# Block sums of the two right-hand operands made and split early, kept in DRAM, and loaded by GpSimd's queue

## The chip, the cores and the metric

The kernel runs on one core of one Trainium2 chip. The metric is the device time of one execution in microseconds (us). TensorE (PE) does the matmuls, and its weight loads are listed apart as PEld; VectorE is DVE, ScalarE is ACT, GpSimd is POOL, and SyncE (SP) does little but issue DMAs. DMAs issued from SP go to a hardware queue, those issued from GpSimd to a software queue; GpSimd also computes.

## The reference, cut to what matters

One layer of a hybrid block on 1024 tokens of 1024 channels, all in float32:

```python
h = rms_norm(x, norm_g)
z = h @ w_in                       # 1024 x 9216: q, k, v, gate of retention; q, k, v, gate of
                                   # differential attention; two merge gates mg_r, mg_d
o_r = rms_norm(retention(q_r, k_r, v_r), ret_norm_g) * silu(gate_r)      # chunks of 128
o_d = rms_norm(diff_attention(qd, kd, v_d), sub_norm_g) * silu(gate_d)   # causal, ALiBi
m = sigmoid(mg_r) * (o_r @ ret_w_o) + sigmoid(mg_d) * (o_d @ diff_w_o)
out = x + m @ w_out
```

## The kernel before, in words

**Split operands.** A float32 matrix is used in matmuls as two parts in the type float32r, a high part (an ACT copy) and a low part (a DVE subtraction of the high part from the original). `split` and `cut` make them; each takes one ACT and one DVE instruction for 128 x 512 numbers. A product is the sum of three passes, high x high, high x low and low x high, so one `product` of 128 x 512 results over 512 rows is 4 x 3 = 12 matmuls.

**The order of stages.** The normalised input, transposed, stays in SBUF as `hT`, four tiles `hq[kh, f]` (kh: which half of the 1024 channels, f: which half of the tokens), each of 128 partitions x 4 row blocks x 2 parts x 512 tokens (16 KB per partition). Then come the projections `rqk0`, `rv0`, `rqk1`, `rv1` of the retention (two groups of four heads, eight token tiles each), with the retention's own small matmuls put between them by hand (`after` gives an item a tick and a weight, `among` lays it between the parts of a projection). After these come the eight heads of the attention in the same manner, with the projections of the gates begun beside them (`first_duo`). Then follow three groups of large products: the gate projections of `h` (16 pairs), the two branch projections `y` (`ret_w_o`, then `diff_w_o`), and the output projection `out` with `w_out`.

**The large products** save matmuls by a scheme with sums of blocks. The right-hand operand R is seen as 2 x 2 blocks r11, r12, r21, r22, and these are used instead of them:

```python
t1 = r11 + r12;  t3 = r12 + r22;  t2 = r22 + t1;  t4 = t2 + r21
```

Each of these is a split tile of the size of an `hq`. Seven products are made for each pair of output strips: two "firsts" (with r11 and r21) and five "rests" (with t2, t3, t1, then t4 and r22). For the gates R is `hT`; for `y0` and `y1` it is the gated branch output `og`, read from DRAM; for `out` it is `w_out`. A dictionary `RB` holds the tiles in use, and `HOME` gives each a fixed place: r11, t3, r21, r22 lie where the four `hq` were, and t1, t2, t4 in a pool `act2`, which is opened when the attention's pools are closed. So there is one place for each name, and a new tile waits until the old one has been read for the last time.

`late_r(name, src)` makes the t tiles from DRAM through staging tiles, or, with no `src` (the gates), from the two parts of the `hq` in place. `early_r` loads and splits r11 and r21. `firsts` and `rests` run the products; `Pair.prep` loads a pair's left operand (two raw tiles of the tag `wraw`, three buffers), makes four sums of its blocks on DVE and splits them. For a strip of `y`, `done_y` loads the gate `s` (and, in the last pair of the second branch, the running sum `m`), both through two buffers of the tag `ld`, multiplies, and either stores to `md` from SP or accumulates into `md` by a DMA from GpSimd's queue. The firsts of `out` read `md` back (`rf_out`).

**The order on each engine** is set by a planner that simulates the program before it is built: it fills each engine's and each queue's list in the order in which instructions become ready in its simulation, earlier program lines first. Each engine and each queue then takes its list strictly in order. So instructions of `out` stand among those of `y1`, where their inputs allow it.

In the retention `r_qkT`, `r_kv`, `r_state`, `r_score`, `r_o` and `r_out` handle one tile of 128 tokens of four heads; the values `v` of a tile have eight buffers, the squares `sq` two.

Of the kernel before, what the change touches and what calls it, by code (L numbers as in the profile page):

```python
# [9 lines left out]
F32 = mybir.dt.float32  # L10
F32R = mybir.dt.float32r
AF = mybir.ActivationFunctionType
ALU = mybir.AluOpType
AX = mybir.AxisListType

P = 128
# [46 lines left out]
def tile_hybrid_block(ctx, tc, x, norm_g, w_in, ret_norm_g, ret_w_o, dq_g, dk_g,  # L63
                      lq1, lk1, lq2, lk2, sub_g, diff_w_o, w_out, consts, out):
    nc = tc.nc
    x, w_in, out = x[0], w_in[0], out[0]
    ret_w_o, diff_w_o, w_out = ret_w_o[0], diff_w_o[0], w_out[0]
# [4 lines left out]
    dram = ctx.enter_context(tc.tile_pool(name="dram", bufs=1, space=bass.MemoryType.DRAM))  # L72
    wpool = ctx.enter_context(tc.tile_pool(name="wpool", bufs=NWS))
    gp = ctx.enter_context(tc.tile_pool(name="gp", bufs=3))
# [6 lines left out]
    def split(t, src):  # L81

        n = src.shape[-1]
        nc.scalar.activation(t[:, 0, :n], src, AF.Copy)
        nc.vector.tensor_tensor(t[:, 1, :n], src, t[:, 0, :n].bitcast(F32), ALU.subtract)
# [94 lines left out]
    md = [dram.tile([P, 4, S], F32, name=f"md{kh}") for kh in range(2)]  # L180
    first = [dram.tile([P, 2, 512], F32, name=f"first{q}") for q in range(16)]


    def cols(c, n):
        return w_in[:, c:c + n]
# [35 lines left out]
    def first_duo(q, following):  # L221

        banks = [pst("pj", f"fb{q + i}") for i in range(2)]
        for kh in range(2):
# [13 lines left out]
    hq = {(q, f): act.tile([P, 4, 2, 512], F32R, tag=f"r{q}{f}", name=f"hT{q}{f}")  # L238
          for f in range(2) for q in range(2)}
    hT = {(k, f): hq[k // 4, f][:, k % 4] for f in range(2) for k in range(NK)}  # L240

    def proj(chunk, t, n=512):
        if t == 3:
            wnext(chunk)
        z = pst("pj", f"z_{chunk}_{t}")
        step(z[:, :n], [hT[k, t // 4] for k in range(NK)], slice((t % 4) * P, (t % 4 + 1) * P),
             W[chunk], slice(0, n))
        return z

    with tc.tile_pool(name="rq", bufs=8) as rq, ExitStack() as early:  # L250
# [34 lines left out]
        R = {}  # L285

        def qk_unit(g, t):
            z = proj(f"rqk{g}", t)
            qk = rq.tile([P, 512], F32, tag="qk", name=f"qk{g}{t}")
            nc.vector.tensor_tensor(  # L290
                qk.rearrange("p (a b) -> p a b", b=64), z.rearrange("p (a b) -> p a b", b=64),
                qkdec[:, g, :].unsqueeze(2).broadcast_to([P, 8, 64]), ALU.mult)
            R[g, t] = dict(qk=qk)
            tick()
# [10 lines left out]
        rp = early.enter_context(tc.tile_pool(name="rp", bufs=2))  # L305
# [30 lines left out]
        nc.vector.tensor_tensor(nlam, ls[:, 3:4], ls[:, 2:3], ALU.subtract)  # L336
        nc.vector.tensor_scalar(nlam, nlam, -LAM_INIT, None, ALU.add)

        def r_qkT(g, t):
            c = R[g, t]  # L340
            tp = pst("tr", f"qkTp{g}{t}", NTR)
            for j in range(4):
                nc.tensor.transpose(tp[:, j * P:(j + 1) * P], c["qk"][:, j * P:(j + 1) * P], ident)

            qz = c["qz"] = qzs[t % 3]
            for e in range(2):
                b = slice(64 * e, 64 * e + 64)
                nc.scalar.activation(qz[b, e::2, :], tp[b, :256].rearrange("p (a b) -> p a b", b=P),
                                     AF.Copy)
            kT = c["kT"] = rp.tile([P, 2, 256], F32R, tag="kT", name=f"kT{g}{t}")  # L350
            split(kT, tp[:, 256:])
            qs = c["qs"] = rp.tile([P, 2, 512], F32R, tag="qs", name=f"qs{g}{t}", bufs=QSB)
            qf = qz.rearrange("p a b -> p (a b)")
            nc.scalar.activation(qs[:, 0, :], qf, AF.Copy)
            nc.gpsimd.tensor_tensor(qs[:, 1, :], qf, qs[:, 0, :].bitcast(F32), ALU.subtract)
# [41 lines left out]
        def r_o(g, t):  # L397
            c = R[g, t]
            o = pst("s", f"ro{g}{t}")
            for h in range(4):  # L400
                hsl = slice(h * P, (h + 1) * P)
                nc.tensor.matmul(o[:, hsl], c["sT"][:, h, :], c["v"][:, hsl],
                                 start=True, stop=(t == 0))
                if t > 0:
                    nc.tensor.matmul(o[:, hsl], c["qz"][:, h, :],
                                     R[g, t - 1]["state"][:, h // 2, :], start=False, stop=True)
            sq = rp.tile([P, 4, P], F32, tag="sq", name=f"rsq{g}{t}")
            nc.scalar.activation(sq.rearrange("p a b -> p (a b)"), o, AF.Square)
            ss = rp.tile([P, 8], F32, tag="ss", name=f"rss{g}{t}")
            nc.vector.tensor_reduce(ss[:, :4], sq, AX.X, ALU.add)  # L410
            rstd(ss[:, 4:], ss[:, :4], rp, f"r{g}{t}", 4, 1.0 / P)
            o1 = c["o"] = rp.tile([P, 4, P], F32, tag="o1", name=f"ro1{g}{t}")
            nc.vector.tensor_tensor(o1, o.rearrange("p (a b) -> p a b", b=P),
                                    ss[:, 4:].unsqueeze(2).broadcast_to([P, 4, P]), ALU.mult)
# [12 lines left out]
        for g in range(2):  # L427
            if g > 0:
                for t in range(NT):
                    qk_unit(g, t)  # L430
            for t in range(NT):
                z = proj(f"rv{g}", t)
                if t == 0:
                    group_consts(g)
                v = R[g, t]["v"] = rp.tile([P, 512], F32, tag="v", name=f"v{g}{t}", bufs=8)
                nc.scalar.activation(v, z, AF.Copy)
                after(1, .46, lambda a=(g, t): r_qkT(*a))
                if t < NT - 1:
                    after(1, .01, lambda a=(g, t): r_kv(*a))
                    after(2, .64, lambda a=(g, t): r_state(*a))  # L440
                after(2, .64, lambda a=(g, t): r_score(*a))
                after(3, 1.72, lambda a=(g, t): r_o(*a))
                after(5, .46, lambda a=(g, t): r_out(*a))
                tick()
# [14 lines left out]
    with tc.tile_pool(name="dp", bufs=2) as dp:  # L459
# [175 lines left out]
        for q in range(4, 12, 2):  # L635
# [14 lines left out]
                t1=(act2, "t1"), t2=(act2, "t2"), t4=(act2, "t4"))  # L650

    def new_r(which, name):
        pool, tag = HOME[which]
        RB[which] = pool.tile([P, 4, 2, 512], F32R, tag=tag, name=f"{which}_{name}")
        return RB[which]
# [5 lines left out]
    def cut_r(which, j, src):  # L661
        t = RB[which]
        cut(t[:, j, 0, :], t[:, j, 1, :], src)

    def add(dst, a, b, op=ALU.add):
        nc.vector.tensor_tensor(dst, a, b, op)  # L666

    def stage(name):
        return lpool.tile([P, 512], F32, tag="rs", name=name, bufs=7)

    def whole(which, j):

        return RB[which][:, j, 0, :].bitcast(F32), RB[which][:, j, 1, :].bitcast(F32)

    def early_r(name, src):

        for which, kh in (("r11", 0), ("r21", 1)):
            new_r(which, name)
            for j in range(4):
                r = stage(f"{which}_{name}{j}")  # L680
                nc.sync.dma_start(r, src(kh, j, 0))
                cut_r(which, j, r)

    def late_r(name, src):

        for n in ("t2", "t1", "t4"):
            new_r(n, name)
        if src:
            new_r("t3", name)
        for j in range(4):  # L690
            r11, r12, r22 = (stage(f"{n}_{name}{j}") for n in ("r11s", "r12s", "r22s"))
            for r, kh, f, which in ((r11, 0, 0, "r11"), (r12, 0, 1, "t3"), (r22, 1, 1, "r22")):
                if src:
                    nc.sync.dma_start(r, src(kh, j, f))
                else:
                    add(r, *whole(which, j))
            add(r11, r11, r12)
            add(r12, r12, r22)
            add(r22, r22, r11)
            cut_r("t2", j, r22)  # L700
            cut_r("t3", j, r12)
            cut_r("t1", j, r11)
        if src:
            new_r("r22", name)
        for j in range(4):
            t = stage(f"t4_{name}{j}")
            if src:
                r22 = stage(f"r22t_{name}{j}")
                nc.sync.dma_start(t, src(1, j, 0))
                nc.sync.dma_start(r22, src(1, j, 1))  # L710
                h, l = whole("t2", j)
                add(t, t, h)
                add(t, t, l)
            else:
                add(t, *whole("t2", j))
                for half in whole("r21", j):
                    add(t, t, half)
            cut_r("t4", j, t)
            if src:
                cut_r("r22", j, r22)  # L720

    def run(parts):
        for part in parts:
# [167 lines left out]
    def o_src(br):  # L891
        return lambda kh, j, f: og[br][kh][:, j, f * 512:(f + 1) * 512]

    late_r("h", None)
    first_duo(12, lambda: more(14, 15))
    pairs = [gate_pair(q) for q in range(16)]
    first_duo(14, pairs[0].prep)
# [29 lines left out]
        rests([Pair(f"y{br}{p}", srcs[p], lambda t=p1[p]: t, done_y(p)) for p in range(4)])  # L927


    def w_src(kh, j, f):  # L930
        return w_out[(4 * kh + j) * P:(4 * kh + j + 1) * P, f * 512:(f + 1) * 512]

    def m_src(i):
        def src(kh, s0, n):
            return md[kh].rearrange("p j (s i n) -> p j s i n", s=2, i=4)[:, :, s0:s0 + n, i, :]
# [11 lines left out]
    def first_out(i, b):  # L947
        done_out(i)(0, 0, temp("c", f"c11_out{i}"), b)

    early_r("w", w_src)  # L950
    p1 = firsts("out", [m_src(i) for i in range(4)], first_out)
    late_r("w", w_src)
    rests([Pair(f"out{i}", m_src(i), lambda t=p1[i]: t, done_out(i)) for i in range(4)])


# [24 lines left out]
```

## Time and profile before

| what | value |
|---|---|
| median of 3 runs (lowest, highest) | 1325.26 us (1324.67, 1328.49) |
| the profiled execution | 1325.96 us, of which its span is 1324.2 us |
| mean granted clock of TensorE over the span | 0.985 of full |
| PE busy / DVE busy / ACT busy / POOL busy | 1260.6 / 954.6 / 647.4 / 265.3 us |
| moved by DMA | 171.01 MB, mean 129 GB/s |
| of that on SP's queue / on GpSimd's queue | 165.78 MB / 3.95 MB |

Busy time is the time in which an engine executes; matmuls overlap their neighbours, so a busy PE is not a PE at its peak. The stages on the span's clock, about: norm and `rqk0` to 72 us, the retention to 290, the attention to 794, the gates from there, `y0` and `y1` until 1240, `out` to the end. "DMA share" is the mean busy share of the core's 16 DMA engines in a stretch.

### The profile page before, as it was taken

To read this page: it belongs to the slowest core of one execution; us is meant where nothing else is said; L and a number is where in the kernel's file an instruction comes from. 1 tells how busy PE (TensorE), PEld (TensorE's weight loads), DVE (VectorE), ACT (ScalarE), POOL (GpSimd) and SP (SyncE) were. 2 spreads that over 40 slices of the span, in tenths; PEclk is the share of its full clock that TensorE was granted. 3 is DMA by queue.
4 is the path that set the end of the run, shared out by engine and by line. 5 is a ranking of instruction groups with operands and counts; after the bars stand their busy time and mean duration, and the time that the engine had idled before them with its cause. 6 is when DMAs were issued, how large, how long until landed. Compare 5 with 4: busy or idle time off the path is not lost. (4 is left out here: it accounts for less than half of the span.)

```text
span 1324.2 us, 19831 instructions
## 1 busy us (share of the span) xinstructions
PE 1260.6 (95%) x6836; PEld 1112.0 (84%) x6836; DVE 954.6 (72%) x2020; ACT 647.4 (49%) x1448; POOL 265.3 (20%) x367
## 2 busy tenths in 40 slices
PE   7999999999999999999999995999989999999598
PEld 5888888889999999999999884787767777778487
DVE  7436435736786878778686849987665799998884
ACT  6235123527575766757576633433433554333430
POOL 3134113323342524334242100000000000011000
PEclk9999999999999999999999998999999999999799
DMA  7212120331020201202020544687655768979864
GB/s 258 59 37 72 57 72 8 116 115 49 1 65 9 56 15 51 64 1 65 9 72 9 169 158 159 219 279 242 208 189 170 248 213 265 324 208 256 255 199 144
DMA packets 158262, 171.01 MB, mean 129 GB/s; under 512 B 9920, under 2 KB 108368, under 8 KB 158160
## 3 DMA queue, kind: packets, MB, share of 16 engines
q1 hardware_dynamic: 155904, 165.78, 39.1%
q0 software_dynamic: 2256, 3.95, 2.0%
q8 instruction: 54, 0.88, 0.3%
q14 instruction: 48, 0.39, 0.1%
HBM read 123.55 MB, written 46.14 MB: 128 GB/s over the span
## 5 line engine op out<-in xcount | busy, mean ns | idle before, releaser
L121 PE MATMUL z_d<-w_d,hT 128*128 128x384 f32 x1536 | 300.7, 340 | 0.7 <-DVE nsq L486 0.7
L121 PEld LDWEIGHTS z_d<-w_d,hT 128*128 128x128 f32 x1536 | 264.2, 188 | 2.8 <-DVE nsq L486 1.0
L537 ACT ACTIVATE S<-S,ast 128x256 f32<-128x256 f32 (+7 forms) x128 | 98.7, 772 | 29.2 <-DVE ast L533 27.6
L531 PE MATMUL sps<-K,Q 128*128 128x512 f32 (+5 forms) x384 | 107.9, 364 | 0.3 <-ACT Q L512 0.3
L121 PE MATMUL z_rv<-w_rv,hT 128*128 128x512 f32 x384 | 98.8, 398 | 0.0
L918 POOL DMA_DIRECT2D md<-c_y x12 | 10.5, 872 | 433.4 <-DVE c_y L909 422.3
L121 PE MATMUL z_rqk<-w_rqk,hT 128*128 128x512 f32 x384 | 95.0, 401 | 1.4 <-ACT hT L281 1.4
L130 PE MATMUL fb<-hT,fw 128*128 128x512 f32 x384 | 94.3, 396 | 0.9 <-ACT ft L229 0.9
L121 PEld LDWEIGHTS z_rqk<-w_rqk,hT 128*128 128x128 f32 x384 | 71.6, 192 | 16.3 <-ACT hT L281 2.0
L130 PEld LDWEIGHTS fb<-hT,fw 128*128 128x128 f32 x384 | 70.3, 188 | 14.9 <-ACT ft L229 1.1
L571 PE MATMUL dops<-V,aTs 128*128 128x128 f32 x576 | 81.8, 276 | 0.0
L571 PEld LDWEIGHTS dops<-V,aTs 128*128 128x128 f32 x576 | 78.5, 191 | 2.6
L121 PEld LDWEIGHTS z_rv<-w_rv,hT 128*128 128x128 f32 x384 | 68.7, 188 | 11.7
L533 DVE CUSTOM_DVE_ANT_0 S<-sps,ndist 128x512 f32<-128x512 f32 (+5 forms) x128 | 67.5, 534 | 5.1 <-PE sps L531 4.7
L91 POOL TENSOR_TENSOR nss<-ms_n,mh 128x4 f32<-128x4 f32 x64 | 65.9, 1029 | 4.1
L531 PEld LDWEIGHTS sps<-K,Q 128*128 128x128 f32 x384 | 63.3, 190 | 2.2 <-ACT Q L512 0.9
L488 POOL TENSOR_TENSOR nsq<-nsq,gh 128x256 f32<-128x256 f32 x64 | 50.2, 788 | 73.4 <-DVE nsq L486 62.0
L130 PE MATMUL y_h<-t_h,ls_h 128*128 128x512 f32 x192 | 48.6, 401 | 15.1 <-ACT ls_h L658 15.1
L130 PE MATMUL w_h<-t_h,l_h 128*128 128x512 f32 x192 | 48.6, 404 | 10.0 <-DVE u_h L823 9.1
L548 DVE SCALAR_TENSOR_TENSOR S<-S,ast,S 128x128 f32<-128x128 f32 (+3 forms) x64 | 56.6, 884 | 1.3
L130 PEld LDWEIGHTS y_h<-t_h,ls_h 128*128 128x128 f32 x192 | 37.1, 194 | 23.9 <-ACT ls_h L658 15.5
L130 PEld LDWEIGHTS w_h<-t_h,l_h 128*128 128x128 f32 x192 | 36.3, 192 | 20.8 <-DVE u_h L823 12.1
(246 smaller groups left out, 2721.5 us busy)
## 6 DMA issues: line engine op xcount, KB each, us to landing
wr_d<-in_w_in_dram SPq DMA_DIRECT2D x96, 128.0 KB, 2.7
fr<-in_w_in_dram SPq DMA_DIRECT2D x16, 512.0 KB, 4.4
first<-ft SPq DMA_DIRECT2D x32, 256.0 KB, 2.2
ra_h<-in_w_in_dram SPq DMA_DIRECT2D x16, 512.0 KB, 3.6
rb_h<-in_w_in_dram SPq DMA_DIRECT2D x16, 512.0 KB, 5.1
s<-sg SPq DMA_DIRECT2D x32, 256.0 KB, 4.4
og<-c_h SPq DMA_DIRECT2D x24, 256.0 KB, 3.3
sg<-c_h SPq DMA_DIRECT2D x24, 256.0 KB, 3.2
```

The source lines that it names most:

```text
L91: nc.gpsimd.tensor_tensor(out_t, ms, mh[:, :n], ALU.pow)
L121: nc.tensor.matmul(o, a[k][:, i0, asl], b[k][:, i1, bsl], start=(k == 0 and j == 0), stop=(k == NK - 1 and j == 2))
L130: nc.tensor.matmul(bank, L[:, i0, j * P:(j + 1) * P], R[:, j, i1, :], start=(start and j == 0 and i == 0), stop=(j == 3 and i == 2), skip_ ...
L488: nc.gpsimd.tensor_tensor(sq, sq, hd["g"], ALU.mult)
L531: nc.tensor.matmul(sp[:, :m], hd["Q"][t][:, j, e, :], hd["K"][:, j, c], start=(e == 0), stop=(e == 1))
L533: nc.vector.tensor_tensor_reduce(sb[:, c], sp[:, :m], ndist[:, S - n + m * f:S - n + m * f + m], -slope, FMAX if f == 0 else st[:, j:j + 1 ...
L537: nc.scalar.activation(sb[:, :n], sb[:, :n], AF.Exp, bias=st[:, j:j + 1], scale=-1.0, accum_out=st[:, 2 + j:3 + j])
L548: nc.vector.scalar_tensor_tensor(S0[:, :n], S1[:, :n], st[:, 6:7], S0[:, :n], ALU.mult, ALU.add)
L571: nc.tensor.matmul(o[:, :P], aT[:, b, :], hd["V"][f][:, b, :], start=(kb == 0), stop=(kb == t))
L918: nc.gpsimd.dma_start(m, t, accum_op=ALU.add)
```

## The change

The sums t1 to t4 of `hT`, and all seven right-hand tiles of `w_out`, are made during the retention by a new function `r_ahead`. For each row block `j` it makes the sums on DVE in float32, splits each (ACT and DVE) into one of three buffers of the tag `oq`, and stores the 512 KB from GpSimd's queue into a DRAM tile `ahead`. `hT` is handled beside `rv0` (after the token tiles 1, 3, 5 and 7), `w_out` beside `rqk1`; the raw blocks of `w_out` are loaded by SP. Where the tiles are used, `load_r` loads them from DRAM by GpSimd's queue, two DMAs of 1 MB for a tile. `late_r` is now for `og` alone and `early_r` for `og` alone; the `hT` sum t3 gets a tile of its own at its home and is no longer written over `hq[0, 1]`. To make room, `v` has five buffers and `sq` one. The diff, with lines left out that only follow from this:

```diff
+    ahead = {(n, w): dram.tile([P, 4, 2, 512], F32R, name=f"{w}_{n}")
+             for w, ns in (("h", ("t1", "t2", "t3", "t4")),
+                           ("w", ("r11", "r21", "r22", "t1", "t2", "t3", "t4"))) for n in ns}
...
+        op = early.enter_context(tc.tile_pool(name="op", bufs=2))
+
+        def put(n, w, j, src):
+            o = op.tile([P, 2, 512], F32R, tag="oq", name=f"oq_{w}{n}{j}", bufs=3)
+            split(o, src)
+            nc.gpsimd.dma_start(ahead[n, w][:, j], o)
+
+        def r_ahead(w, j):
+            def tt(o, a, b):
+                nc.vector.tensor_tensor(o, a, b, ALU.add)
+            def raw(n, j):
+                if n == "r21":
+                    return op.tile([P, 512], F32, tag="or", name=f"or_{n}{j}", bufs=1)
+                return gp.tile([P, 512], F32, tag="gt", name=f"or_{w}{n}{j}", bufs=3)
+            q = {}
+            for n, (kh, f) in dict(r11=(0, 0), r12=(0, 1), r22=(1, 1), r21=(1, 0)).items():
+                if w == "w":
+                    q[n] = raw(n, j)
+                    nc.sync.dma_start(q[n], w_out[(4 * kh + j) * P:(4 * kh + j + 1) * P,
+                                                  f * 512:(f + 1) * 512])
+                    if n != "r12":
+                        put(n, w, j, q[n])
+                elif n != "r21":
+                    q[n] = raw(n, j)
+                    tt(q[n], *(hq[kh, f][:, j, i, :].bitcast(F32) for i in range(2)))
+            tt(q["r11"], q["r11"], q["r12"])
+            put("t1", w, j, q["r11"])
+            tt(q["r12"], q["r12"], q["r22"])
+            put("t3", w, j, q["r12"])
+            tt(q["r22"], q["r22"], q["r11"])
+            put("t2", w, j, q["r22"])
+            for r in ([q["r21"]] if w == "w" else [hq[1, 0][:, j, i, :].bitcast(F32) for i in range(2)]):
+                tt(q["r22"], q["r22"], r)
+            put("t4", w, j, q["r22"])
...
-            sq = rp.tile([P, 4, P], F32, tag="sq", name=f"rsq{g}{t}")
+            sq = rp.tile([P, 4, P], F32, tag="sq", name=f"rsq{g}{t}", bufs=1)
...
                     qk_unit(g, t)
+                    if t % 2 == 1:
+                        r_ahead("w", t // 2)
             for t in range(NT):
                 z = proj(f"rv{g}", t)
+                if g == 0 and t % 2 == 1:
+                    r_ahead("h", t // 2)
...
-                v = R[g, t]["v"] = rp.tile([P, 512], F32, tag="v", name=f"v{g}{t}", bufs=8)
+                v = R[g, t]["v"] = rp.tile([P, 512], F32, tag="v", name=f"v{g}{t}", bufs=5)
...
+    def load_r(name, which, queue):
+        for n in which:
+            t = new_r(n, name)
+            for j in range(0, 4, 2):
+                queue.dma_start(t[:, j:j + 2], ahead[n, name][:, j:j + 2])
...
-    late_r("h", None)
+    load_r("h", ("t3", "t2", "t1", "t4"), nc.gpsimd)
...
-    early_r("w", w_src)
+    load_r("w", ("r11", "r21", "t2", "t3", "t1", "t4", "r22"), nc.gpsimd)
     p1 = firsts("out", [m_src(i) for i in range(4)], first_out)
-    late_r("w", w_src)
     rests([Pair(f"out{i}", m_src(i), lambda t=p1[i]: t, done_out(i)) for i in range(4)])
```

More of the change, by code (lines that the diff above doesn't have):

```diff
@@ L684, in late_r @@
     def late_r(name, src):
-        for n in ("t2", "t1", "t4"):
+        for n in ("t2", "t3", "t1", "t4"):
             new_r(n, name)
-        if src:
-            new_r("t3", name)
         for j in range(4):
             r11, r12, r22 = (stage(f"{n}_{name}{j}") for n in ("r11s", "r12s", "r22s"))
[L692 to L696, printed above, removed]
+            for r, kh, f in ((r11, 0, 0), (r12, 0, 1), (r22, 1, 1)):
+                nc.sync.dma_start(r, src(kh, j, f))
             add(r11, r11, r12)
@@ L702, in late_r @@
             cut_r("t1", j, r11)
-        if src:
-            new_r("r22", name)
+        new_r("r22", name)
         for j in range(4):
[L706 to L717, printed above, removed]
-            cut_r("t4", j, t)
-            if src:
-                cut_r("r22", j, r22)
+            t, r22 = stage(f"t4_{name}{j}"), stage(f"r22t_{name}{j}")
+            nc.sync.dma_start(t, src(1, j, 0))
+            nc.sync.dma_start(r22, src(1, j, 1))
+            for half in whole("t2", j):
+                add(t, t, half)
+            cut_r("t4", j, t)
+            cut_r("r22", j, r22)
+    def load_r(name, which, queue):
[3 more added lines that the diff above has]
+                queue.dma_start(t[:, j:j + 2], ahead[n, name][:, j:j + 2])
     def run(parts):
@@ L927, in tile_hybrid_block @@
         rests([Pair(f"y{br}{p}", srcs[p], lambda t=p1[p]: t, done_y(p)) for p in range(4)])
-    def w_src(kh, j, f):
-        return w_out[(4 * kh + j) * P:(4 * kh + j + 1) * P, f * 512:(f + 1) * 512]
     def m_src(i):
```

## The prediction

> **What bounds the kernel now.** I read the totals of the page first, then TensorE's longest waits, then the stages around those waits in the timeline and in busy time by stretches, and last the chain that ended last. Totals:
>
> ```profile
> span 1324.2 us, 19831 instructions
> PE 1260.6 (95%) x6836; PEld 1112.0 (84%) x6836; DVE 954.6 (72%) x2020; ACT 647.4 (49%) x1448; POOL 265.3 (20%) x367
> ```
>
> TensorE is idle for 63.6 us of the span, so a change that removes no matmul can win only from that and from matmuls run at a lowered clock. The waits of TensorE (engine, line, whom it waited for: us in total, times, longest) say where it sits:
>
> ```profile
> PE y_h L130 <- ACT ls_h L658: 15.1, 1, 15.1
> PE X_out L130 <- ACT la_out L658: 14.3, 1, 14.3
> ```
>
> Two single waits hold 29.4 us of that. The first wait lies where the block sums of hT are made. Timelines there (start, duration, engine, line, what), of PE:
>
> ```profile
> 790.85 22.18 PE L130 MATMUL fb<-hT,fw 128*128 128x512 f32 x96
> 828.10 1.22 PE L130 MATMUL y_h<-t_h,ls_h 128*128 128x512 f32 x2 [15.07 <-ACT ls_h L658]
> ```
>
> Of DVE:
>
> ```profile
> 794.21 0.69 DVE L666 TENSOR_TENSOR r11s_h<-hT 128x512 f32<-128x512 f32 x1 [2.82 <-DMA ot_d<-doT]
> ...
> 824.30 0.68 DVE L666 TENSOR_TENSOR s_h<-ra_h,rb_h 128x512 f32<-128x512 f32 x1
> ```
>
> Of SP's queue:
>
> ```profile
> 781.50 0.38 SPq L748 DMA_DIRECT2D rb_h<-in_w_in_dram  x1
> ```
>
> The raw weights of gate pair 0 were requested by 781.50, but the first sum made of them (s_h) runs at 824.30: from 794.21 DVE works through the 52 instructions of the hT sums first. TensorE ends its last first-product at 813.03 and stands still for 15.07 us. Busy time by stretches (columns: PE, PEld, DVE, ACT, POOL busy with counts, granted clock, DMA share, GB/s):
>
> ```profile
> 0.00:24.00 24.00, 15.17 (x62) 12.26 (x63) 14.31 (x24) 14.43 (x25) 6.71 (x17) 1.00 0.93 334
> 72.00:144.00 72.00, 72.00 (x433) 63.03 (x433) 40.92 (x76) 30.62 (x66) 27.46 (x27) 1.00 0.16 48
> 144.00:192.00 48.00, 48.00 (x235) 40.27 (x234) 15.46 (x23) 7.48 (x13) 3.69 (x5) 1.00 0.23 66
> 192.00:290.00 98.00, 97.35 (x572) 85.68 (x571) 52.99 (x97) 38.34 (x83) 31.75 (x37) 1.00 0.27 81
> 794.00:814.00 20.00, 19.03 (x84) 15.22 (x82) 19.79 (x33) 9.64 (x15) 0.00 (x0) 1.00 0.57 186
> 814.00:828.00 14.00, 0.00 (x0) 0.00 (x0) 14.00 (x25) 4.03 (x7) 0.00 (x0) 0.60 0.32 111
> 828.00:836.00 8.00, 7.88 (x22) 5.80 (x23) 8.00 (x14) 3.25 (x7) 0.00 (x0) 0.63 0.42 133
> 836.00:860.00 24.00, 24.00 (x108) 19.87 (x107) 23.12 (x39) 12.13 (x21) 0.00 (x0) 1.00 0.77 245
> 1224.00:1251.00 27.00, 13.14 (x58) 10.53 (x57) 25.09 (x42) 10.46 (x19) 0.90 (x2) 0.80 0.87 255
> 1251.00:1266.00 15.00, 14.59 (x52) 11.48 (x53) 11.25 (x20) 6.50 (x12) 0.00 (x0) 0.80 0.80 237
> ```
>
> In the gap DVE is busy 14.00 of 14.00 us while PE does nothing: DVE is the bound there. The clock falls in the gap, and 828 to 836 holds 22 matmuls; at the pace of 836 to 860 (108 in 24 us, 0.222 us each) these take 4.9 us, so the slow restart costs 3.1 us more and the place loses **18.2 us**. In the same way 1251 to 1266 holds 52 matmuls worth 11.6 us, so the second wait (14.3 us) costs 3.4 us more, **17.7 us** in all. During the retention (72 to 290) PE is busy without a break and DVE, ACT and DMA are not full.
>
> **The change part by part.** *Removed at 794:* the hT sums, per block row 9 and 4 DVE instructions, 52 in all, and 16 ACT copies. *Removed at the end:* 28 loads of 256 KB from SP, 28 ACT copies, and 48 DVE instructions (28 subtractions, 20 additions). *Added in the retention:* for hT 48 DVE, 16 ACT and 16 stores of 512 KB on GpSimd's queue; for w_out 44 DVE, 28 ACT, 28 such stores, and 16 loads of 256 KB from SP. *Added later, on GpSimd's queue:* 8 loads of 1 MB (hT) and 14 (w_out). The price of one (groups of instructions: busy us, mean ns of one | idle before):
>
> ```profile
> L659 DVE TENSOR_TENSOR ls_h<-s_h,ls_h 128x512 fp32r<-128x512 f32 x64 | 43.2, 682 | 0.3
> ...
> L658 ACT ACTIVATE ls_h<-s_h 128x512 fp32r<-128x512 f32 x64 | 38.3, 620 | 11.8 <-DVE s_h L666 8.3 <-PE z_h L130 2.8 <-ACT ls_h L658 0.6
> ```
>
> Transfers, with median us from issue to landing:
>
> ```profile
> first<-ft SPq DMA_DIRECT2D x32, 256.0 KB, 2.2
> ...
> s<-sg SPq DMA_DIRECT2D x32, 256.0 KB, 4.4
> ...
> md<-c_y POOLq DMA_DIRECT2D x12, 256.0 KB, 6.6
> ```
>
> The issue of one on GpSimd's queue:
>
> ```profile
> 1229.78 0.86 POOL L918 DMA_DIRECT2D md<-c_y  x1 [5.75 <-DVE c_y L909]
> ```
>
> *Retention.* Added DVE: 48 x 0.68 = 33 us for hT in 72 to 144, 44 x 0.68 = 30 us for w_out in 144 to 192. The rows leave 31 and 33 us idle there, and 45 us after. DVE becomes nearly full, but its total is below the time. ACT gets 10 and 17 us into 41 and 41 idle; GpSimd 44 issues x 0.86 = 38 us into 45 + 44. The stores wait for one of three slots: copy 0.62, subtraction 0.68, issue 0.86, landing about 2.9 (2.2 for 256 KB on SP, and 0.7 more for the second half at full rate) make 5.1 us for three puts, so 28 puts take 47 us of the 48 in which w_out is handled. If a landing is the 6.6 us of GpSimd's accumulating stores, it is 8.8 us for three, 82 us for 28, and ACT and DVE, which take instructions in order, hold back the copies that empty TensorE's two projection banks. The cover is matmuls with no gap and the free time after 192. A gain is excluded, as PE has no idle time there. I take **+2 us**, nearer to the plain store of 2.2 us than to an accumulation; ends 0 and +12. The smaller number of v and square buffers costs nothing: a chunk's v is read for the last time three steps later, and five remain.
>
> *hT loads.* t3's home is free when the last projection of the attention has run, so it comes in ahead. t2, t1 and t4 take memory that the attention frees at about 794.2 (the DMA that ended DVE's wait there). Rate: the busiest stretch moved 334 GB/s at a share of 0.93, 359 at a full one; SP takes 186 in 794 to 814, so 173 is left. The three tiles of 2.1 MB then land at 806, 818.5 and 831. With DVE free the sums s_h run at about 795 instead of 824. PE, in order, wants t2 at 813.0, t3 at 815.7, t1 at 818.4, and t4 after the second pair's first product, at 823.7: t1 is just in time, and **what is late next is t4**, by 7 us. With the full 359 GB/s nothing is late; with SP at the 245 of 836 to 860, 114 is left, t4 lands at 849.5, and 25.8 us are lost instead of 18.2. I take a wait of 4 us, between the first two, as SP's stores of the first products before 814 can yield: **-14 us**; ends -18 and +8.
> The Trainium skill (DMA: Bandwidth & Descriptors, Anatomy of one DMA — SWDGE (gpsimd) path) fits a DMA issued from GpSimd by 2.0 us plus bytes over 436 GB/s. An estimate from that page alone puts all six loads down by 811, with no wait left, and the sum 4 us lower; no stretch of this trace moved that much, so the sum stays with its rows.
>
> *The boundary to the output product.* The chain that ended last:
>
> ```profile
> 1214.19 7.97 DMA s<-sg
> ...
> 1242.49 4.66 DMA md<-c_y
> 1247.23 3.48 DMA rf_out<-md
> ```
>
> SP's queue:
>
> ```profile
> 1229.52 0.33 SPq L913 DMA_DIRECT2D m<-md  x1
> ...
> 1236.85 0.42 SPq L913 DMA_DIRECT2D m<-md  x1
> ...
> 1242.49 0.33 SPq L916 DMA_DIRECT2D md<-c_y  x1
> ```
>
> X_out waits for a row of transfers, not only for DVE: s lands after 7.97 us (median 4.4), I infer behind w_out's own loads, which SP issues around it; then m is loaded (1229.52), used, the next m (1236.85), the sum stored (1242.49), read back (1247.23). Two buffers of the tag "ld" set that order, and it stays. What goes is the traffic of w_out on SP (3.6 us at s) and w_out's instructions between those of the row on DVE, some two (1.4 us): **-5 us**. The loads that replace it are 14.7 MB against 7.3, on another queue, most of them free to start only when the last pair has read the tile before. The better end is -11: from 1229.52 to 1242.49 the row takes 13 us for two m loads and their sums, and 6 us of it could go as well. The worse is +6: the five transfers of the row each 1.2 us longer. An accumulation on GpSimd's queue now stands behind any load issued ahead of it that waits for its tile; the read-back of md waits for that accumulation. r11 and r21 are free early and can go ahead.
>
> *The second branch (1100 to 1192):* their 4.2 MB then fall where DMA is busy already; **+1 us**, ends 0 and +4 (4.2 MB at 359 GB/s is 12 us, a third of it on the path).
>
> **Sum:** 1325.96 (the profiled execution; 1324.2 of span and 1.8 around it) + 2 - 14 - 5 + 1 = 1310. The median of the runs, 1325.26, lies 0.7 lower, so **1310** stands.
>
> **The rivals.** *Stores hold the retention:* the three slots are the bound. For it: 28 puts need 47 of 48 us even at the short landing; against it: DVE and PE have free work after 192. Price 12 instead of 2: 1320. *The boundary gains nothing:* the row of transfers is as long as before or longer under GpSimd's loads. For it: the share is 0.87 there already; against it: SP loses 28 transfers. -5 becomes +4: 1319. *GpSimd's loads starve, and the kernel is slower:* place t4 of hT, price +8 instead of -14: 1332. It decides from where the three tiles get less than 132 GB/s (6.3 MB by 841.9, when the 18.2 us are used up). For it: 245 GB/s on SP as soon as the gate pairs run; against it: pairs 0 and 1 then have their raw weights already.
> The Trainium skill (SBUF — State Buffer, SBUF: two separate sides) names another way to that starvation: a DVE instruction that takes both ports locks GpSimd out of writing its descriptors. The trace does not bear it out so far: the issue at 1229.78 took 0.86 us while DVE was busy 25.09 of 27.
>
> **How the numbers follow.** The forecast (1300 to 1318) has 0.60, the retention 0.14, the boundary 0.14, the starved loads 0.12. A run of this kernel tells 0.3% (4 us) from no change: faster is below 1321.3, slower above 1329.2. Faster: 0.60 + 0.08 + 0.10 = 0.78; same 0.06 + 0.03 + 0.02 = 0.11; slower 0.01 + 0.10 = 0.11. The range leaves out most of the starved case and the far good end (-18 and -11 with nothing lost elsewhere would be 1297): 1299 to 1325.
>
> **What would show it.** Right: the 15 us wait of y_h is gone or below 7 us, s_h stands near 795, no stretch of half clock near 816 to 836; PE is still full between 72 and 290; X_out's wait is about 9 us. Wrong: z_h or w_h waiting for t1 or t4 by more than 10 us; PE waiting for qk L290 or for a put's slot before 290; m, s or rf_out landing later than before; accumulations held on GpSimd's queue.

## The result, and the profile after

The changed kernel takes **1346.03 us** (median, 1342.81 to 1346.53) against 1325.59 beside it: ratio **1.0145** [1.0123, 1.0168], 20.4 us slower. The forecast was 1310, with a range up to 1325. The profiled execution spans 1344.6 us against 1324.2. The totals of its page:

```profile
span 1344.6 us, 19995 instructions
...
PE 1270.0 (94%) x6836; PEld 1116.2 (83%) x6836; DVE 953.4 (71%) x2012; ACT 647.0 (48%) x1448; POOL 304.4 (23%) x433
```

TensorE's idle time rose from 63.6 to 74.6 us, and the rest of the loss is matmuls that ran longer (busy 1260.6 before, 1270.0 now). Three groups of matmuls tell the place. They are the last projections of the retention, the first product of the stage `y0` behind the gates, and `out`'s first product (line, what, count: duration ns min/median/max, first and last start us). Before:

```profile
L121 PE MATMUL z_rv<-w_rv,hT x384: 386/390/482, 64.1 to 247.5; 128*128 128x512 f32 x192
...
L130 PE MATMUL X_y<-r_o,la_y x192: 387/389/390, 1064.3 to 1167.3; 128*128 128x512 f32 x192
...
L130 PE MATMUL X_out<-r_w,la_out x96: 387/389/794, 1220.7 to 1265.0; 128*128 128x512 f32 x96
```

After:

```profile
L121 PE MATMUL z_rv<-w_rv,hT x384: 387/389/481, 64.3 to 251.2; 128*128 128x512 f32 x192
...
L130 PE MATMUL X_y<-r_o,la_y x192: 388/389/792, 1069.0 to 1178.4; 128*128 128x512 f32 x192
...
L130 PE MATMUL X_out<-r_w,la_out x96: 388/389/792, 1240.7 to 1284.9; 128*128 128x512 f32 x96
```

The lag is 3.7 us when the projections end (251.2 against 247.5), 4.7 when X_y starts, 20.0 when X_out starts, and no more behind it. So: retention **+3.7**, the attention and the gates **+1.0** where 14 were to be won, `y0` and `y1` up to X_out **+15.3** where 4 were to be won. X_y's own stretch grew by 6.4 of these (109.4 against 103.0).

TensorE's waits after (whom it waited for: us in total, times, longest):

```profile
PE X_out L130 <- ACT la_out L704: 16.7, 1, 16.7
PE y_h L130 <- ACT ls_h L704: 11.0, 1, 11.0
...
PE w_y L130 <- DVE u_y L862: 6.2, 2, 6.0
...
PE X_y L130 <- ACT p_y L834: 4.3, 1, 4.3
```

Both waits of before are still there, and two new ones stand beside them. The y_h wait has another cause now. DVE's timeline:

```profile
800.09 0.69 DVE L712 TENSOR_TENSOR s_h<-ra_h,rb_h 128x512 f32<-128x512 f32 x1 [5.50 <-DMA ot_d<-doT]
...
826.90 0.69 DVE L712 TENSOR_TENSOR s_h<-ra_h,rb_h 128x512 f32<-128x512 f32 x1 [19.98 <-DMA rb_h<-in_w_in_dram]
```

SP's queue there, and rb_h's landing times:

```profile
802.46 0.38 SPq L787 DMA_DIRECT2D rb_h<-in_w_in_dram  x1
```

```profile
DMA to landing us min/median/max: 3.5/5.3/24.4
```

The landing times of rb_h before:

```profile
DMA to landing us min/median/max: 3.5/5.1/7.3
```

DVE is free as forecast: pair 0's first sum stands at 800.09, not 824.30. But then it waits 19.98 us for pair 1's raw weights (rb_h is the second of a pair's two raw tiles), which were issued at 802.46 and took 24.4 us; before, the slowest rb_h took 7.3. What SP's queue got meanwhile is in the queues' totals of 810 to 818 us (packets, MB, share of 16 engines; q0 is GpSimd's queue, q1 is SP's):

```profile
q0 software_dynamic: 375, 2.71, 84.3%
q1 hardware_dynamic: 375, 0.56, 22.3%
```

Equal counts of packets, and five times the bytes for GpSimd: its loads run at 339 GB/s, SP's transfers at 70. The raw weights starve, not the loads.

### The profile page after: what moved, and what is told of

The parts are those of the page before. It is cut to its first block, busy times and chain, and to the rows that moved or that the text cites. A ratio compares the mean times of both kernels' runs of the same rounds, so it can differ in the third digit from the quotient of the medians.

```text
span 1344.6 us, 19995 instructions
## 1 busy us (share of the span) xinstructions
PE 1270.0 (94%) x6836; PEld 1116.2 (83%) x6836; DVE 953.4 (71%) x2012; ACT 647.0 (48%) x1448; POOL 304.4 (23%) x433
## 5 line engine op out<-in xcount | busy, mean ns | idle before, releaser
L759 POOL DMA_DIRECT2D r_w<-w_r x6 | 3.5, 646 | 362.5 <-PE X_y L130 357.7
L704 ACT ACTIVATE ls_h<-s_h 128x512 fp32r<-128x512 f32 x64 | 38.4, 619 | 32.7 <-DVE s_h L712 28.5
## 6 DMA issues: line engine op xcount, KB each, us to landing
t_h<-h_t POOLq DMA_DIRECT2D x8, 1024.0 KB, 13.3
```

Of the source, the lines that this page charges most:

```text
L704: nc.scalar.activation(dst_hi, src, AF.Copy)
L759: queue.dma_start(t[:, j:j + 2], ahead[n, name][:, j:j + 2])
```

## The experiments

The theories in their expectations: A, a DMA engine serves the queues in turn, one packet each whatever its size; B, queues share bytes; C, accumulations stand behind loads on GpSimd's queue; D, it is not the queue. Each time is compared with runs of the kernel before that were taken beside it. The table gives for each kernel the ratio to it and, from the profiled execution, the lag behind the profile of before at the three places above and at the end of the span (us); one profile scatters by some 3 us (bufs, whose time is unchanged, shows +2.7 at one place).

| kernel | ratio, 95% interval | z_rv ends | X_y starts | X_out starts | span |
|---|---|---|---|---|---|
| the change | 1.0145 [1.0123, 1.0168] | +3.7 | +4.7 | +20.0 | +20.4 |
| run2k | 1.0145 [1.0119, 1.0171] | +4.6 | +6.2 | +23.1 | +24.0 |
| run512 | 1.0265 [1.0235, 1.0294] | +4.0 | +18.9 | +36.3 | +39.0 |
| sp_queue | 1.0017 [1.0005, 1.0029] | +4.9 | -1.4 | +2.5 | +4.5 |
| stores | 1.0021 [1.0005, 1.0038] | +4.1 | +7.4 | +6.1 | +5.8 |
| bufs | 1.0000 [0.9986, 1.0014] | -0.6 | +1.2 | +2.7 | +0.7 |
| h_only | 0.9979 [0.9962, 0.9996] | +0.5 | +0.5 | +1.6 | +1.4 |
| h_act | 1.0002 [0.9987, 1.0018] | -0.5 | -0.7 | -0.8 | -0.9 |
| **h_sp** | **0.9931** [0.9905, 0.9958] | -0.1 | -8.1 | -8.8 | -8.9 |
| w_only | 1.0136 [1.0109, 1.0164] | +2.9 | +3.2 | +20.2 | +20.3 |
| w_sp | 1.0060 [1.0043, 1.0076] | +2.9 | +4.2 | +7.8 | +9.9 |
| w_sp_late | 1.0067 [1.0052, 1.0082] | +2.8 | +1.8 | +6.6 | +8.6 |
| both_late | 1.0029 [1.0017, 1.0041] | +3.6 | -2.3 | +1.8 | +3.5 |

**turns: two queues alone.** A kernel that leaves the layer's computation out: in most of its eight phases GpSimd issues six loads of 1 MB in runs of one length, and SP at the same time three of 512 KB in runs of 1 KB (in one phase 4 KB).

> A kernel of transfers alone, with the layer's computation left out: in eight phases SP loads three times 512 KB, while GpSimd's queue loads six times 1 MB in runs of 8, 4, 2 or 0.5 KB or nothing. Theory A (each DMA engine serves the queues in turn, one descriptor each, whatever its size): the first 512 KB of SP, in runs of 1 KB, 32 descriptors per engine, lands after about 4 us alone, 15 beside runs of 8 KB (32 x 0.40 + 2), 9 beside 4 KB, 6.5 beside 2 KB, 4.6 beside 0.5 KB; with SP's own runs at 4 KB beside 8 KB after about 6. Rival B (the queues share the bytes evenly): 5 to 6 us beside any of them.

The queues' totals while both are at work, with 8 KB runs on GpSimd and 1 KB runs on SP (44 to 52 us):

```profile
q0 software_dynamic: 400, 2.88, 87.5%
q1 hardware_dynamic: 400, 0.41, 14.8%
```

400 packets each, and seven times the bytes: A, and not B. With 4 KB runs on SP the counts are again equal, 103 and 105, and the bytes 0.84 and 0.43 MB (141 to 144 us). The landing times that A named can't be compared: beside 8 KB runs SP's first load landed after 3.7 us and not 15, as GpSimd's loads start later; the last of its three took 15.9. And the phases with runs of 4, 2 and 0.5 KB all moved GpSimd's 6.29 MB in 1632 packets, some 4 KB each, so shorter packets are not tried here.

**run2k, run512: shorter runs.** The whole change, with GpSimd's loads in runs of 2 KB or 512 bytes. The second:

```diff
-            for j in range(0, 4, 2):
-                queue.dma_start(t[:, j:j + 2], ahead[n, name][:, j:j + 2])
+            for c in range(0, 512, 128):
+                queue.dma_start(t[:, :, :, c:c + 128], ahead[n, name][:, :, :, c:c + 128])
```

> The changed kernel with the loads of the ready tiles cut into runs of 2 KB (four DMAs of 512 KB for a tile instead of two of 1 MB with runs of 8 KB); bytes, queue and moment of issue stay. Theory A: SP's loads of raw weights and of m are no longer held up (24.4 us at worst becomes under 10, m 8.8 becomes 5 to 6), the 11 us wait of y_h goes, X_out's 16.7 shrinks: 1318 to 1330. Rival B (bytes) and rival C (accumulations stand behind loads on GpSimd's queue): 1341 to 1349, as the changed kernel.

> The same with runs of 512 B (four DMAs of 512 KB, each a quarter of all columns). Theory A: SP is held up still less, but the loads themselves get slower: SP's worst rb_h under 8 us, t_h landing 15 to 25 us, 1316 to 1332. Rivals B and C: 1341 to 1352.

1347.44 and 1363.01 us: the gain that A named did not come in either, run2k lies where rivals B and C put it, and run512 above all the ranges. C is out all the same: in the changed kernel the accumulations on GpSimd's queue wait for DVE's results and not for a load, and land after 5.3 us (median; 6.6 before). B does not fit the counts. The turns are there: with 2 KB runs the counts are 905 and 904 in 810 to 818 us, and run512 has in the same stretch:

```profile
q1 hardware_dynamic: 1364, 1.90, 79.8%
q0 software_dynamic: 1424, 0.72, 45.5%
```

Now SP's packets are the larger ones and it gets 1.90 of 2.61 MB; its slowest rb_h lands in 9.4 us. But the tiles t_h take up to 29.7 us instead of 23.4, and TensorE waits 15.4 us at z_h. With 2 KB runs rb_h still takes 13.3 us at most and t_h 20.0; the 11 us wait of y_h goes (1.1), but z_h and fb wait longer. The moment of issue did not stay, however, as the expectation had it: GpSimd now issues eight of the twelve loads and then waits, before each of the last four, until an earlier one has landed. The last goes out at 818.34 with 2 KB runs and at 832.16 with 512 B, against 803.2 in the changed kernel. In run512:

```profile
832.16 0.87 POOL L759 DMA_DIRECT2D t_h<-h_t  x1 [3.71 <-DMA t_h<-h_t]
```

```profile
841.23 5.46 PE L130 MATMUL z_h<-t_h,ls_h 128*128 128x512 f32 x12 [15.38 <-issue]
```

The profile names nobody for the wait at z_h; that it is for these late pieces fits, but is not shown. So the share of the queues decides who is late, but these two runs don't say what a fairer share alone would be worth. The next run tries an order instead: the tiles and pair 1's weights in one queue.

**sp_queue: one queue for all.** The loads of both parts are issued by SP, so they stand in the order of issue with the other transfers (both sides are then named as plain float32, the same bytes).

```diff
-    load_r("h", ("t3", "t2", "t1", "t4"), nc.gpsimd)
+    load_r("h", ("t3", "t2", "t1", "t4"), nc.sync)
...
-    load_r("w", ("r11", "r21", "t2", "t3", "t1", "t4", "r22"), nc.gpsimd)
+    load_r("w", ("r11", "r21", "t2", "t3", "t1", "t4", "r22"), nc.sync)
```

> The changed kernel with the loads of the ready tiles issued by SP in 1 MB DMAs instead of by GpSimd. Theory A: no turns between two queues any more; a transfer waits only for what SP issued before it: 1320 to 1335. Rival B: 1341 to 1349, the bytes are the same. Rival C: the accumulations on GpSimd's queue are free of the loads: 1330 to 1338, with rb_h as late as in the changed kernel.

1329.65 us: the queue alone is worth some 17 of the 20 us. The slowest rb_h lands in 12.0 us. The profile is 4.9 us behind when the projections end and 4.5 at the end of the span, so the retention loses about what is left.

**stores, bufs: the retention.** stores makes and stores all blocks but loads none (the later stages work as before). bufs is the kernel before with the two rings shortened alone:

```diff
-            sq = rp.tile([P, 4, P], F32, tag="sq", name=f"rsq{g}{t}")
+            sq = rp.tile([P, 4, P], F32, tag="sq", name=f"rsq{g}{t}", bufs=1)
...
-                v = R[g, t]["v"] = rp.tile([P, 512], F32, tag="v", name=f"v{g}{t}", bufs=8)
+                v = R[g, t]["v"] = rp.tile([P, 512], F32, tag="v", name=f"v{g}{t}", bufs=5)
```

> All blocks of hT and w_out are made, split and stored as in the changed kernel, but nothing of it is loaded: the later stages make their operands as before. It prices the retention alone. Theory A (the retention's DVE is full, the projections end 3.9 us later, and everything behind is as before): 1329 to 1331, with the first gate's last product about 4 us later than before. Rival D (the lag is made up in the attention, where TensorE has slack): 1325 to 1327. Rival C2 (half the loss is in the stores' queue and the shrunk rings, and goes on): over 1334.

> The kernel before with only the two rings of the retention shortened as the change shortens them (v from 8 to 5 buffers, the squares from 2 to 1). Theory A (the 3.6 us of the retention are VectorE's extra 64 instructions for w_out, ahead of the ones that TensorE waits for): no loss, 1325 to 1328. Rival R (the shortened rings hold the retention): 1329 to 1331, with the projections' last product about 4 us later.

stores takes 1331.66 us against 1328.07; by the ratio that is 2.8 us more, within 0.7 and 5.0, and just above theory A's 1329 to 1331. Busy time in two stretches of it (columns as in the prediction: PE, PEld, DVE, ACT, POOL):

```profile
96.00:120.00 24.00, 23.30 (x150) 20.46 (x150) 23.01 (x39) 13.36 (x28) 14.04 (x20) 1.00 0.80 270
120.00:144.00 24.00, 21.14 (x130) 18.04 (x128) 21.95 (x38) 14.00 (x29) 11.21 (x14) 1.00 0.84 281
```

and TensorE's waits from 80 to 270 us:

```profile
PE sc L433 <- DVE ro L455: 2.0, 2, 1.3
PE sc L433 <- POOL qs L397: 1.4, 1, 1.4
```

The same stretches of bufs:

```profile
96.00:120.00 24.00, 24.00 (x152) 21.15 (x151) 13.88 (x28) 10.05 (x23) 10.24 (x11) 1.00 0.08 23
120.00:144.00 24.00, 24.00 (x152) 21.25 (x151) 18.06 (x31) 11.51 (x24) 9.18 (x8) 1.00 0.41 121
```

The rings cost nothing that shows (1.0000). The loss is TensorE's 3.6 us in 96 to 144, where w_out's blocks raise DVE from 31.9 to 45.0 of 48 us and TensorE waits for DVE and GpSimd. (The blocks of w_out are 44 DVE instructions in all, not the 64 that the expectation of bufs names.) ACT waits in the same stretch for slots that a store has not yet freed:

```profile
ACT oq_wt L84 <- DMA w_r<-oq_wr: 3.0, 1, 3.0
ACT oq_wr L84 <- DMA w_t<-oq_wt: 1.1, 3, 0.6
```

From 144 to 192 it waits 15.2 us more for slots, but there TensorE waits for nothing. No run tells what part of the 3.6 us the stores have, through ACT, and what part DVE's order. The +7.4 of stores where X_y starts, 3.3 above its lag in the retention, is not explained; theory A expected nothing there. The kernels without w_out's blocks in the retention (h_only, h_act, h_sp) have no lag there, so hT's blocks, which run in 51 to 101, are free.

**h_only, h_sp, h_act: hT's part, by three queues.** w_out's part is as before; only the queue of the eight loads differs (`nc.gpsimd`, `nc.sync`, `nc.scalar`).

> Only the hT part of the change, w_out's part as before, loads on GpSimd's queue. Theory A (the loads take eight bytes for each one or two of SP's transfers, pair 1's raw weights land late): the retention loses under 1 us, since in the changed kernel the loss stands in 96 to 144 us, where w_out's blocks are made; the hT stage gains about nothing because rb_h lands over 15 us late: 1324 to 1328. Rival D (the hT stage gains its 14 us as the prediction had it, and w_out's part ate it): 1311 to 1315.

> As h_only, with the four loads' eight DMAs issued by SP, so that they stand in SP's own queue behind the raw weights that were issued before them. Theory A: the raw weights of pair 1 land in under 13 us, the long wait of y_h goes, and the stage gains the 6 us that the kernel with all loads on SP's queue showed between the retention and the first gate's last product: 1317 to 1322. Rival D (it is not the queue but what is late next, the sums of the raw weights on DVE): as h_only within 2 us.

> As the kernel with hT's part alone on SP's queue, but ScalarE issues the eight loads, so they stand in a third queue. Theory A (a DMA engine takes one descriptor of each queue in turn, and 8 KB ones beside SP's 0.5 and 1 KB ones take most of the bytes, whatever queue they are in): rb_h of pair 1 lands over 15 us late again, and the time is that of the loads on GpSimd's queue, 1322 to 1328. Rival S (it is something of GpSimd's queue alone, such as its descriptors made by software): as with SP's queue, 1315 to 1320, with rb_h at most 12 us.

1324.66, 1318.0 and 1327.91 us, each as theory A had it. On ScalarE's queue the picture is GpSimd's; 806 to 814 us (q10 is ScalarE's queue):

```profile
q10 hardware_dynamic: 400, 2.88, 86.4%
q1 hardware_dynamic: 404, 0.42, 15.1%
```

rb_h takes up to 20.7 us with ScalarE's queue and 22.7 with GpSimd's. So it is not something of the software queue; it is the same with either of the two second queues tried. In one queue (h_sp) it takes 11.8, and TensorE's waits of before at y_h are gone:

```profile
PE X_out L130 <- ACT la_out L701: 15.4, 1, 15.4
PE w_h L130 <- DVE u_h L859: 10.6, 6, 3.1
...
PE z_h L130 <- DVE c_h L847: 7.2, 5, 3.0
PE fb L130 <- ACT ft L232: 3.5, 1, 3.5
```

This kernel beats both, by 0.7% the one before. It wins some 9 us, not 18: y_h's 15.1 us are gone, but z_h waits 3.6 us more than before, w_h 1.5 and fb 2.6 (0.9 before).

**w_only, w_sp, w_sp_late, both_late: w_out's part.** w_sp has SP issue its loads; w_sp_late puts those of t2, t3, t1, t4 and r22 behind `firsts` in the program, where the reads of md are written; both_late is w_sp_late with h_sp's part.

```diff
-    load_r("w", ("r11", "r21", "t2", "t3", "t1", "t4", "r22"), nc.sync)
+    load_r("w", ("r11", "r21"), nc.sync)
     p1 = firsts("out", [m_src(i) for i in range(4)], first_out)
+    load_r("w", ("t2", "t3", "t1", "t4", "r22"), nc.sync)
```

> Only w_out's part of the change, hT's as before, loads on GpSimd's queue. Theory A: +3 to +4 in the retention, then +12 to +16 behind the hT stage, where m, s and rf_out wait behind the loads' descriptors: 1341 to 1346, nearly the whole of the loss. Rival D (the loss comes of the hT stage's disorder, carried on): 1328 to 1333.

> Only w_out's part of the change, its loads issued by SP at the place where the changed kernel issues them. Theory A: the retention's 3.6 us stay, and behind the first gate's last product the loss falls from 16 us to about 4, as in the kernel with all loads on SP's queue: 1332 to 1337. Rival B (the 14 MB themselves are too much for this stretch, on any queue): 1342 to 1348.

> As before it, but of the seven blocks only r11 and r21, which X_out uses, are issued ahead of the last product's first part, and t2, t3, t1, t4 and r22 behind its reads of md (rf_out, rb_out) in SP's queue. Theory A (what costs is that the small reads on the way to X_out stand behind or beside the big loads): rf_out lands within 8 us at most, the boundary costs no more than before: 1326 to 1332. Rival B (bytes): the blocks come late, and TensorE waits in the last product instead: 1335 to 1345.

> Both parts, all loads on SP's queue, w_out's t2, t3, t1, t4 and r22 behind the reads of md. If the parts add up: 9 us won at hT's sums, 3.6 lost in the retention, and what the boundary then gives or takes (-4 to +4): 1318 to 1326, so not under the kernel with hT's part alone.

w_only takes 1346.60 us, just above A's 1341 to 1346: w_out's part alone is the whole loss, 3 us in the retention and 17 between X_y and X_out. One stall of it, followed through w_only's timelines. GpSimd issues two loads, SP reads a piece of md:

```profile
1218.58 1.36 POOL L777 DMA_DIRECT2D t_w<-w_t  x2
```

```profile
1220.12 3.04 SPq L840 DMA_DIRECT2D rf_out<-md  x3
```

ACT and DVE, each in its order, wait for that read:

```profile
1230.73 1.36 ACT L701 ACTIVATE la_out<-rf_out 128x512 fp32r<-128x512 f32 x2 [20.66 <-DMA rf_out<-md]
```

```profile
1217.59 0.68 DVE L877 TENSOR_TENSOR u_y<-y_y,p_y 128x512 f32<-128x512 f32 x1
1231.39 0.69 DVE L702 TENSOR_TENSOR la_out<-rf_out,la_out 128x512 fp32r<-128x512 f32 x1 [13.11 <-ACT la_out L701]
```

and TensorE for DVE's next sum behind it:

```profile
1235.68 5.46 PE L130 MATMUL w_y<-t_o,l_y 128*128 128x512 f32 x12 [7.73 <-DVE u_y L880]
```

The read of 256 KB takes 10.5 us; before, rf_out's median was 4.1 and DVE's longest wait of this kind 2.4. Meanwhile (1220 to 1230.6 us) the queues moved:

```profile
q0 software_dynamic: 498, 2.46, 76.2%
q1 hardware_dynamic: 1560, 0.87, 29.5%
```

The counts are not equal here, also not in favour of SP while the loads run (1220 to 1228 us: 475 packets for GpSimd's queue, 221 for SP's), so this stretch shows SP's queue held to 82 GB/s beside 232, not the rule itself. On SP's queue the same 14 loads cost 4 us in place of 17 up to X_out (7.8 - 4.2 against 20.2 - 3.2): w_sp is at 1334.62, as A had it. w_sp_late (1335.08) is no better and missed its 1326 to 1332, although rf_out lands within 7.3 us. It is within rival B's 1335 to 1345, but TensorE's wait there is X_out's 18.7 us for la_out, made from md, and none names a block, as B would have it. The edit did not move the loads where it matters. The planner sets the order of SP's queue, and around the read of m it is the same in both. w_sp:

```profile
1225.33 0.91 SPq L777 DMA_DIRECT2D t_w<-w_t  x2
1226.88 0.32 SPq L970 DMA_DIRECT2D m<-md  x1
1227.25 1.32 SPq L777 DMA_DIRECT2D t_w<-w_t  x2
```

w_sp_late:

```profile
1224.15 0.91 SPq L777 DMA_DIRECT2D t_w<-w_t  x2
1225.71 0.32 SPq L970 DMA_DIRECT2D m<-md  x1
1226.07 1.18 SPq L777 DMA_DIRECT2D t_w<-w_t  x2
```

In the chain that ended last in w_sp_late, the two reads of m are the longest waits on the way to X_out:

```profile
1225.71 12.05 DMA m<-md
...
1238.94 10.64 DMA m<-md
```

Before, a read of m took 7.1 us at most. So whether the rest of the loss is the place of the loads, ahead of m in SP's queue, or the bytes themselves, twice those of before, stays open: no run moves them behind m, and none takes bytes away alone. both_late (1330.36) missed its range too; it has the order of sp_queue around m and, within the noise, its time. With w_out's part added, h_sp loses its gain.

## Why the prediction was wrong, point by point

- **Retention, +2 (0 to +12):** 3.7 in the profile of the change, 2.8 by the ratio of stores. The size is near; the place is not. I put hT's blocks in 72 to 144 and w_out's in 144 to 192; they ran in 51 to 101 and 99 to 177, and TensorE waited for DVE's and GpSimd's next instructions although DVE's total fitted. The rival *stores hold the retention* did not come at its price of 12: ACT waits for slots, most of it after 144, where TensorE does not wait. What share of the 3.7 is the stores' is open.
- **hT loads, -14 (-18 to +8): the step that failed.** "SP takes 186 in 794 to 814, so 173 is left" treats SP's traffic as a first claim and GpSimd's as the remainder. The runs show the reverse: equal packets, 339 GB/s for GpSimd, 70 for SP. Therefore what was late next was not t4 but pair 1's rb_h, which I had counted as loaded ("pairs 0 and 1 then have their raw weights already"). They can't have them: the tag `wraw` has three buffers for two tiles a pair, so pair 1's second tile is requested only when pair 0's sums have read one. The profile of before shows it, behind the sum at 824.30:

```profile
828.01 0.38 SPq L748 DMA_DIRECT2D rb_h<-in_w_in_dram  x1
```

With DVE free it moved up to 802.46, among the loads of t_h, which GpSimd issued from 800.51. Measured: +1.0 instead of -14. Even in the best queue it is -8.1, as the next waits take up half of the stall.
- **The boundary, -5 (-11 to +6), and the second branch, +1 (0 to +4):** +15.3 together. The mechanism behind the worse end was right: the row of small transfers gets longer under the loads. Its price was not: m's median went from 5.1 to 8.8 us and rf_out's, for the reads between 1200 and 1260 us, to 8.9, several in a row, and DVE and ACT stood in order behind them. What I took off, "the traffic of w_out on SP", came back as twice the bytes with the larger share.
- **The rivals:** the slower one, *GpSimd's loads starve*, had the right resource and the wrong victim. *The boundary gains nothing* had the right place at a quarter of its price.
- **By the Trainium skill:** The Trainium skill's estimate (DMA: Bandwidth & Descriptors, Anatomy of one DMA — SWDGE (gpsimd) path) was all six loads down after some 16 us; here they landed in up to 23.4 us each, beside other traffic. The lock of GpSimd by DVE that the Trainium skill (SBUF — State Buffer, SBUF: two separate sides) names shows no sign here: the t_h loads were issued in 535 to 658 ns each. On turns, the Trainium skill (DMA: Bandwidth & Descriptors, Queues, rings and completion order) says that each DMA engine goes round the queues that have work, a packet of several descriptors at a time. The counts here, 375 to 375 and 400 to 400, agree with going round; how many descriptors a turn takes no run here shows.
- **What would show it:** s_h near 795 came true (800.09). y_h below 7 us (11.0), no stretch of half clock (0.54 in 829 to 834), PE full in the retention and X_out at 9 us (16.7) did not, and "m, s or rf_out landing later than before" is what stood there.

## What to carry to other kernels

A second DMA queue is not spare bandwidth: in most stretches here where both had work it took its share by packets, so large transfers moved to it slowed down the small transfers of the first. Put a large prefetch into the queue of the transfers that must come before it, or issue it when none of these is due, and name which small loads fall into its window, also those that the change itself moves there, before counting its gain. Look in the new profile whether an edit of the order changed the order. A stall removed is worth what the next wait leaves of it, here 8 of 15 us.

## What the runs showed of the hardware

- Two queues at work got equal counts of packets: 375 and 375 (8 KB loads beside SP's), 400 and 404 on ScalarE's queue, 400 and 400, 103 and 105 with nothing else running, 905 and 904 in run2k, 1424 and 1364 in run512. In w_only (1220 to 1228 us) they did not: 475 and 221, which stays open.
- With large packets the 16 engines moved more than I had extrapolated (359 GB/s): 3.28 MB in the 8 us from 810 to 818 is 409 GB/s.
- With packets of 512 B on GpSimd's queue less was moved: in run512, 2.61 MB in the same 8 us is 327 GB/s.
